# New product orders, held first reads, a third seven-product pair in the output projection, and the residual put into PSUM ahead of the products, in a two-layer decoder kernel

## The chip, the cores and the metric

The kernel runs on one core of a Trainium2 chip. The metric is the device time of one execution in microseconds; lower is better. Five engines are named in the profile: PE (TensorE, the matrix products, with its weight loads as PEld), DVE (VectorE), ACT (ScalarE), POOL (GpSimd) and SP (SyncE, which only issues DMA here). Each engine takes its instructions in order.

## What is computed

Two identical layers act on x, 256 rows (tokens) by 2048 columns, all in float32. Cut to what matters:

```
def hybrid_layer(x, ...):
    h = rms_norm(x, attn_norm)
    proj = h @ w_in                        # 2048 x 6160
    g_q, g_k, g_v, g_gate, g_lr, s_q, s_k, s_v = split(proj)
    o_gla = rms_norm(gla_chunked(g_q, g_k, g_v, gates(g_lr))) * silu(g_gate)
    o_sb  = rms_norm(stick_breaking_attention(rms_norm(s_q), rms_norm(s_k), s_v))
    x = x + concat(o_gla, o_sb) @ w_o      # 2048 x 2048
    hm = rms_norm(x, mlp_norm)
    up = square(relu(hm @ w_up))           # 2048 x 8192
    return x + up @ w_down                 # 8192 x 2048
```

Nearly all arithmetic is in w_in, w_o, w_up and w_down.

## The kernel before

**Three matmuls for one product.** Every float32 operand is split into a high part (rounded to the fp32r format that the matmul takes) and a low part (the value less its high part). A product is high*high + high*low + low*high, so three matmuls of 128x512 columns (lines 1198 to 1200, `product`). For the weights, ACT rounds (line 1066, `whi`) and DVE subtracts (line 1070, `wlo`).

**Units and pairs.** A unit is 1024 output columns (512 for the unit "g"). Its contraction is walked in eight "pairs" of two 128-row blocks. The results of a unit are four 128x512 blocks (two token halves, two column halves), and an ordinary pair takes eight products into PSUM banks 2, 4, 3 and 8. A "fast" pair takes seven, by a Strassen-Winograd scheme into all eight banks (1, 5, 6, 7 as well): it needs sums of weight blocks (DVE, line 858: `ts` and two sums in place in `raw`) and sums of activation blocks (`forms`, lines 454 to 475, tiles `sx`, `sxh`). At the end of a unit its tail folds the banks together: `up_tail` into new tiles, `down_tail` into the residual `xb`.

**The sequence.** Layer 0 begins with a first stretch that is written in the order of program text: x is loaded and turned, and a unit of lines 594 to 615 (`whi`, `wlo`, `acc`) makes the GLA values. Then three units ("iv", "ik", "iq") make projections for layer 0. In each layer follow attention (lines 613 to 1780), then the units g, o 0, o 1, and for q = 0 to 3: up 0, up 1, down 0, down 1. In layer 0 iv, ik and iq of layer 1 come last. All units from iv on are placed by `ordered`.

**How weights come in.** Most pairs come as one 1 MB read that SP issues (line 1002, `raw`, three buffers). The "added" pairs (third entry of an order, two of a unit) come instead in two halves, each read twice by DMAs that POOL issues: line 1033 reads 512 KB into `chi`, rounding on the way (three buffers, `CAST`); ACT writes minus that into `dlo` (line 1037, `negated`, two buffers, `ADDS`); line 1040 reads the same weights again and adds them into `dlo`. So an added half needs no DVE work, one ACT instruction, and two reads. A half is started one half ahead of its use (`AHEAD_BY`).

**What sets the order.** An order is a list of pair numbers, one entry per step (a fast pair has four steps of 2, 2, 2 and 1 products, an ordinary pair two of 4; a half of an added pair is a step of 4), with the fast pairs and the added pairs beside it. PE follows these lists. For the other engines a planner (`Plan`) holds costs and due times: PE pieces are laid end to end, each other piece is due as late as its users allow, and a clock is run in which an engine that is free takes, of the pieces that are ready, the one due first. The order that comes out is the written order of PE, DVE and ACT. The planner's `LAND` is 7.0 for a read and its `ADD` 6.0 for the adding read. The dummy pieces `before` (five PE pieces of twelve matmuls) stand for work ahead of the first unit, and the copies `copy_first` (line 903), which empty the accumulator of the unit before, wait for the fourth of them.

**The lines that the prediction uses.** Line 500 writes the high part of turned x, line 563 is a warming transpose, line 490 turns x, line 334 turns the gains that line 500 scales by, line 1292 applies relu, line 1311 turns the result of an up unit for the down unit.

Of the kernel before, what the change touches and what calls it, by code (L numbers as in the profile page):

```python
# [17 lines left out]
P = 128  # L18
# [1 line left out]
WARM0, WARM1 = 8, 13  # L20
T2 = 5
FAST = (1, 3, 5, 6)
EACH = [0, 0, 1, 1, 1, 1, 2, 3, 3, 3, 3, 2, 5, 5, 5, 5, 4, 6, 6, 6, 6, 4, 7, 7], FAST, (2, 4)
FEWER = [0, 0, 1, 1, 1, 1, 2, 3, 3, 3, 3, 2, 5, 5, 4, 6, 6, 6, 6, 4, 7, 7], (1, 3, 6), (2, 4)
FAST_OF = {"sxh": (0, 1, 3, 5, 6), "sx": FAST}
TWO_WAYS = (("sxh", 0),)
MORE = [0, 0, 0, 0, 2, 1, 1, 1, 1, 2, 3, 3, 3, 3, 4, 5, 5, 5, 5, 4, 6, 6, 6, 6, 7, 7], (0, 1, 3, 5, 6), (2, 4)
# [135 lines left out]
def trunk_kernel(  # L163
# [51 lines left out]
    def act_tile(dt, shape=(P, 4, T)):  # L215
        return apool.tile(list(shape), dt, tag="act", name=nm("act"))
# [29 lines left out]
    def bank(m):  # L246
        return unused.pop(m, None) or new_bank(m)
# [191 lines left out]
    def forms(op, i, t, tag):  # L439

        both = (tag, i) in TWO_WAYS
        keep = tag is None or both

        e = []
        todo = []

        def sums():
            a11, a21, a12, a22 = (t[:, k, r * P : (r + 1) * P] for k in range(2) for r in range(2))  # L450
            n = 4 if keep else 3
            e.append(tmp("t2", [P, 512], bufs=T2)[:, : n * P].rearrange("p (k c) -> p k c", c=P))
# [4 lines left out]
            nc.vector.tensor_tensor(e[0][:, 1, :], a12, e[0][:, 0, :], ALU.subtract)  # L457

        def high():
            if e:  # L460
                if both:
                    op.x[i] = tmp(tag + "k", [P, 4, 2, P], F32R, bufs=1)
                elif keep:
                    op.x[i] = act_tile(F32R, (P, 4, 2, P))
                else:
                    op.x[i] = tmp(tag, [P, 3, 2, P], F32R, bufs=len(FAST))
                todo.append((op.x[i], e[0]))
            if i not in op.t:
                todo.append((op.pair(i), t))
            for d, src in todo:  # L470
                nc.scalar.activation(d[:, :, 0, :], src, AF.Copy)
# [370 lines left out]
    def ordered(l, units, hT, rst, ug, gates_t, mixed=None, ons=None):  # L842
# [22 lines left out]
        def unit_order(u):  # L865

            kind, q, n2 = units[u]
            if kind == "g":
                return [i // 2 for i in range(8)], (), ()
            if kind == "o":  # L870
                pairs = ((4, 5, 6, 7, 0, 1, 2, 3), (4, 5, 6, 0, 7, 1, 2, 3))[n2]
                return [j for j in pairs for _ in range(4 if j < 2 else 2)], (0, 1), ()
            if u and units[u - 1][0] == "down" and kind == "iv":
                return FEWER
            return OWN.get((kind, n2, q), OWN.get((kind, n2), EACH))

        def added(u, j):
# [143 lines left out]
        def rounded(u, j, s):  # L1021

            box = {}
            sl = slice(s * 512, (s + 1) * 512)
            src = weights(u, j)[:, :, sl] if by_columns(u, j) else weights(u, j)[:, s : s + 1, :]

            def flat(key):
                t = box[key].rearrange("p c n -> p (c n)")
                return t.rearrange("p (k n) -> p k n", k=src.shape[1])

            def high():
                box["h"] = tmp("chi", [P, 2, 512], F32R, bufs=CAST)
                nc.gpsimd.dma_start(flat("h"), src)  # L1033

            def negated():
                box["l"] = tmp("dlo", [P, 2, 512], F32R, bufs=ADDS)
                nc.scalar.activation(box["l"], f32(box["h"]), AF.Copy, scale=-1.0)  # L1037
# [46 lines left out]

        last = {}
        sums13 = []
        chi, late, made_halves = [], [], {}
        every = [
            (u, k, j, order[:k].count(j))
            for u in range(len(units))  # L1090
# [15 lines left out]
        def added_steps(u, j):  # L1106

            kind, q, _ = units[u]
            op = {"up": hm, "down": up.get(q)}.get(kind, hT)

            def blk(k, tt):
                sl = slice(tt * P, (tt + 1) * P)
                return lambda: (op.t[j][:, k, 0, sl], op.t[j][:, k, 1, sl])

            for s in range(2):
                if by_columns(u, j):
                    prods = [
                        (m, [(blk(k, tt), k) for k in range(2)])
                        for tt, m in enumerate(((2, 4), (3, 8))[s])
                    ]  # L1120
                else:
                    prods = [
                        (m, [(blk(s, tt), c)])
                        for c, ms in enumerate(((2, 4), (3, 8)))
                        for tt, m in enumerate(ms)
                    ]
                yield prods

        def steps(u, j, is_fast, r, ld, readers):
# [14 lines left out]
                        for tt, m in enumerate((1, 6))]  # L1144
                return

            kept = kind in AHEAD or ({"up": "sxh", "down": "sx"}.get(kind), j) in TWO_WAYS

            def ext(i):
                return lambda: (op.x[j][:, i, 0, :], op.x[j][:, i, 1, :])  # L1150
# [36 lines left out]
                (4, [(blk(1, 1), 0)]),  # L1187
            ]

        def product(m, blocks, box, begin, end):  # L1190

            if begin:
                banks[m] = bank(m)
            for i, (a, c) in enumerate(blocks):
                ah, al = a()
                h, lo = box["h"][:, c], box["l"][:, c]
                o = banks[m]
                nc.tensor.matmul(o, ah, h, start=begin and i == 0, stop=False)
                nc.tensor.matmul(o, ah, lo, start=False, stop=False)  # L1199
                nc.tensor.matmul(o, al, h, start=False, stop=end and i + 1 == len(blocks))  # L1200

        def bk(m):
            return lambda: banks[m]


        def down_tail(u):
# [43 lines left out]
                x_done[2 * n2 + c] = got  # L1250

            return sums, half

        def up_tail(u):
            kind = units[u][0]
# [154 lines left out]
        def turn_gated():  # L1410

            g, cost, turn, a, m, e, high, low, scaled, box = turns.pop(0)
            p = add("PE", cost, turn, a, free[m])
            if e < 2:
                b = add("ACT", A1, scaled, p, take=1)
                free[m] = [b]
                done["o", 0, e] = made(lambda: forms(mixed, e, box[1], "sx"), True, True, b)
            else:
                b = add("ACT", A1, high, p)
                done["o", 0, e] = add("DVE", 0.7, low, b)  # L1420
                free[m] = [b, done["o", 0, e]]
# [30 lines left out]
            gate(0)  # L1452
        for u, (kind, q, n2) in enumerate(units):
            order, quick, by_dma = unit_order(u)
            if kind != "g":
# [9 lines left out]
            for k, j in enumerate(order):  # L1465
# [10 lines left out]
                for m, blocks in prods:  # L1476
                    begin, end = m not in begun, last_use[m] == k
                    begun.add(m)
                    p[m] = add(
                        "PE", 3 * MM * len(blocks),  # L1480
                        lambda a=(m, blocks, box, begin, end): product(*a),
                        h, lo, ready, free[m] if begin else [], opened if u == 0 else [],
                    )
                    for tile_users in users:
                        tile_users.append(p[m])
                if kind == "g" and k == 4 or kind == "o" and n2 == 0 and k == 5:
# [356 lines left out]
```

## Time and profile before

| | |
|---|---|
| time, median of 3 runs | 2147.89 us (2144.24 to 2151.99) |
| the profiled execution's own time | 2145.96 us, span 2144.3 us |
| PE busy | 2124.8 us, 10076 matmuls |
| PEld busy | 1765.1 us |
| DVE busy | 1944.5 us, 2636 instructions |
| ACT busy | 1403.3 us |
| POOL busy | 234.5 us |
| DMA | 488.74 MB, 228 GB/s |
| mean granted TensorE clock | 0.997 |

Busy time is the time in which at least one instruction of the engine was in flight. Matmuls overlap, so a busy PE is not yet a PE that loses nothing: what counts is the distance from one matmul's start to the next. In rows of the timeline the first number is the start in us from the span's start, the second the duration, and the bracket names how long the engine had been idle and what released it. In tables by stretch of time each engine's busy us and count stand under its name, then the granted clock, the share of the DMA engines that was busy, and GB/s.

### The profile page before, as it was taken

To read this page: it belongs to the slowest core of one execution; us is meant where nothing else is said; L and a number is where in the kernel's file an instruction comes from. 1 tells how busy PE (TensorE), PEld (TensorE's weight loads), DVE (VectorE), ACT (ScalarE), POOL (GpSimd) and SP (SyncE) were. 2 spreads that over 40 slices of the span, in tenths; PEclk is the share of its full clock that TensorE was granted. 3 is DMA by queue.
4 is the path that set the end of the run, shared out by engine and by line. 5 is a ranking of instruction groups with operands and counts; after the bars stand their busy time and mean duration, and the time that the engine had idled before them with its cause. 6 is when DMAs were issued, how large, how long until landed. Compare 5 with 4: busy or idle time off the path is not lost.

```text
span 2144.3 us, 28255 instructions
## 1 busy us (share of the span) xinstructions
PE 2124.8 (99%) x10076; PEld 1765.1 (82%) x10076; DVE 1944.5 (91%) x2636; ACT 1403.3 (65%) x1853; POOL 234.5 (11%) x362
## 2 busy tenths in 40 slices
PE   8999999999999999999999999999999999999999
PEld 6788888888888888888888988888888888888887
DVE  5988878999999999999999796699999999999998
ACT  6666666676577566667766575666765765765764
POOL 0110000011111111111111100000111111111110
PEclk9999999999999999999999999999999999999999
DMA  7885365588888988988888644756888888888886
GB/s 247 245 236 179 118 187 196 167 246 252 258 251 246 268 239 253 266 245 238 252 258 251 191 138 137 224 162 204 260 241 258 254 258 247 246 255 256 248 244 196
DMA packets 146992, 488.74 MB, mean 228 GB/s; under 512 B 10298, under 2 KB 19074, under 8 KB 146852
## 3 DMA queue, kind: packets, MB, share of 16 engines
q1 hardware_dynamic: 103076, 327.55, 44.7%
q0 software_dynamic: 43776, 159.40, 31.6%
q8 instruction: 79, 1.29, 0.2%
q14 instruction: 61, 0.50, 0.1%
HBM read 484.81 MB, written 2.10 MB: 227 GB/s over the span
## 4 chain that ended last, share of the span: by engine, by line
PE 55%; issue 36%; POOL 5%; DMA 2%; DVE 1%; ACT 1%; POOLq 0%
POOL dlo L1040 3%; PE acc L613 3%; PE acc L615 2%; PE acc L614 2%; POOL chi L1033 2%; DMA dlo<-in_w_up_dram 1%; DMA dlo<-in_w_in_dram 1%; DMA dlo<-in_w_down_dram 1%; PE ps L1780 0%; DVE wlo L596 0%; DMA chi<-in_w_in_dram 0%; PE ps L724 0%; PE ps L1730 0%; PE ps L1773 0%; PE ps L778 0%
## 5 line engine op out<-in xcount | busy, mean ns | idle before, releaser
L1066 ACT ACTIVATE whi<-raw 128x1024 fp32r<-128x1024 f32 (+1 forms) x701 | 653.2, 955 | 364.6 <-DVE raw L858 209.9
L1070 DVE TENSOR_TENSOR wlo<-raw,whi 128x1024 fp32r<-128x1024 f32 (+1 forms) x701 | 760.9, 1091 | 70.0 <-ACT whi L1066 21.7
L1037 ACT ACTIVATE dlo<-chi 128x1024 fp32r<-128x1024 f32 x152 | 159.9, 1053 | 83.0 <-DMA chi<-in_w_in_dram 13.9
L1066 ACT ACTIVATE whi<-ts 128x1024 fp32r<-128x1024 f32 x165 | 174.4, 1057 | 53.5 <-DVE ts L858 29.2
L858 DVE TENSOR_TENSOR ts<-raw 128x1024 f32<-128x1024 f32 x165 | 200.7, 1216 | 3.9 <-DMA raw<-in_w_down_dram 2.2
L1070 DVE TENSOR_TENSOR wlo<-ts,whi 128x1024 fp32r<-128x1024 f32 x165 | 200.8, 1217 | 0.4 <-PE m__631_2940 L1199 0.2
L613 PE MATMUL acc<-whi,act 128*128 128x512 f32 (+2 forms) x384 | 142.1, 370 | 2.6 <-ACT whi L594 2.6
L615 PE MATMUL acc<-whi,act 128*128 128x512 f32 (+2 forms) x384 | 137.6, 358 | 0.0
L614 PE MATMUL acc<-wlo,act 128*128 128x512 f32 (+2 forms) x384 | 137.4, 358 | 0.0
L594 ACT ACTIVATE whi<-raw 128x1024 fp32r<-128x1024 f32 (+2 forms) x98 | 88.1, 906 | 64.7 <-PE acc L615 64.3
L596 DVE TENSOR_TENSOR wlo<-raw,whi 128x1024 fp32r<-128x1024 f32 (+2 forms) x98 | 100.4, 1030 | 30.4 <-ACT whi L594 29.5
L1033 POOL DMA_DIRECT2D chi<-in_w_up_dram x64 | 35.4, 555 | 759.2 <-PE m__2836_13416 L1200 142.1
L858 DVE TENSOR_TENSOR raw<-raw 128x512 f32<-128x512 f32 x165 | 112.8, 684 | 1.3
L858 DVE TENSOR_TENSOR raw<-ts,raw 128x512 f32<-128x512 f32 x165 | 112.5, 682 | 0.1
L1033 POOL DMA_DIRECT2D chi<-in_w_down_dram x64 | 35.4, 554 | 524.2 <-PE m__3624_17092 L1200 33.1
L1292 ACT ACTIVATE act<-act,st 128x512 f32<-128x512 f32 x88 | 60.5, 715 | 46.5 <-DVE act L858 46.4
L613 PEld LDWEIGHTS acc<-whi,act 128*128 128x128 f32 x384 | 72.9, 190 | 15.3 <-issue 3.4
L615 PEld LDWEIGHTS acc<-whi,act 128*128 128x128 f32 x384 | 72.9, 190 | 10.6
L614 PEld LDWEIGHTS acc<-wlo,act 128*128 128x128 f32 x384 | 73.0, 190 | 9.3 <-DVE wlo L596 0.4
L1040 POOL DMA_DIRECT2D dlo<-in_w_down_dram x64 | 54.7, 854 | 68.4 <-ACT dlo L1037 66.0
L475 DVE TENSOR_TENSOR act<-t,act 128x512 fp32r<-128x512 f32 x90 | 61.1, 682 | 0.0
L1040 POOL DMA_DIRECT2D dlo<-in_w_up_dram x64 | 54.8, 856 | 56.7 <-ACT dlo L1037 55.4
(4156 smaller groups left out, 5738.9 us busy)
## 6 DMA issues: line engine op xcount, KB each, us to landing
raw<-in_w_up_dram SPq DMA_DIRECT2D x96, 1024.0 KB, 7.8
raw<-in_w_down_dram SPq DMA_DIRECT2D x96, 1024.0 KB, 10.0
raw<-in_w_in_dram SPq DMA_DIRECT2D x72, 1024.0 KB, 5.3
chi<-in_w_up_dram POOLq DMA_DIRECT2D x64, 512.0 KB, 5.6
dlo<-in_w_up_dram POOLq DMA_DIRECT2D x64, 512.0 KB, 8.5
raw<-in_w_o_dram SPq DMA_DIRECT2D x32, 1024.0 KB, 5.2
chi<-in_w_down_dram POOLq DMA_DIRECT2D x64, 512.0 KB, 5.9
dlo<-in_w_down_dram POOLq DMA_DIRECT2D x64, 512.0 KB, 10.0
```

Of the source, the lines that this page charges most:

```text
L475: nc.vector.tensor_tensor(d[:, :, 1, :], src, f32(d[:, :, 0, :]), ALU.subtract)
L594: newest["hi"] = nc.scalar.activation(h, r, AF.Copy).ins
L596: newest["lo"] = nc.vector.tensor_tensor(lo[:, q : q + step, :width], r, f32(h), ALU.subtract).ins
L613: nc.tensor.matmul(o, xh[:, sl], whi[:, j, :width], start=first, stop=False)
L614: nc.tensor.matmul(o, xh[:, sl], wlo[:, j, :width], start=False, stop=False)
L615: st["mm"] = nc.tensor.matmul(o, xl[:, sl], whi[:, j, :width], start=False, stop=last).ins
L858: nc.vector.tensor_tensor(dst, a, b, op)
L1033: nc.gpsimd.dma_start(flat("h"), src)
L1037: nc.scalar.activation(box["l"], f32(box["h"]), AF.Copy, scale=-1.0)
L1040: nc.gpsimd.dma_start(flat("l"), src, accum_op=ALU.add)
L1066: nc.scalar.activation(box["h"][:, :n], src(), AF.Copy)
L1070: nc.vector.tensor_tensor(box["l"][:, :n], src(), f32(box["h"][:, :n]), ALU.subtract)
```

## The change

Five things are edited.

- **Orders.** `EACH`, `FEWER` and the lists of up 0, up 1, down 0 and down 1 are written anew, each unit with its own, and `LATER` is new, for ik and iq of layer 1. Fast pairs are interleaved with others, and the added halves are spread differently. The number of fast and of added pairs is as before in all of these units.
- **The output projection.** `O0` and `O1` give the o units three fast pairs (0, 1, 2) in place of two, and two added pairs in place of none.
- **Held first reads.** Ahead of layer 0 the first three `chi` tiles are first touched by ACT (`held_tile`, one column, from `ident`), so their reads wait for that instruction; and in the planner each `chi` read waits for the first product of the unit before its own (`started`). That second edit adds no wait on the chip; it moves the read, and what follows it, in the written order.
- **Seeding.** In down 0, down 1 and o 1 ACT copies the four residual blocks into banks 2, 4, 3 and 8 (`seed`) once the unit before has emptied them; the products are added on top, the first without a start flag. The tail (`seeded_tail`) has eight DVE instructions where `down_tail` had twelve, and five ACT instructions where it had one.
- **Planner costs** are changed by a few per cent.

```diff
-EACH = [0, 0, 1, 1, 1, 1, 2, 3, 3, 3, 3, 2, 5, 5, 5, 5, 4, 6, 6, 6, 6, 4, 7, 7], FAST, (2, 4)
+EACH = [7, 7, 5, 2, 5, 5, 1, 1, 5, 4, 1, 1, 3, 3, 3, 3, 4, 6, 6, 2, 6, 6, 0, 0], FAST, (2, 4)
...
-OWN = {("up", 0): MORE, ("up", 0, 0): EACH}
+O0 = [6, 6, 7, 4, 5, 4, 0, 0, 1, 0, 7, 0, 1, 1, 1, 5, 2, 2, 2, 2, 3, 3], (0, 1, 2), (5, 7)
+O1 = [5, 7, 7, 0, 0, 0, 1, 0, 6, 1, 1, 2, 1, 2, 2, 2, 5, 3, 6, 3, 4, 4], (0, 1, 2), (5, 6)
+SEEDED = (("down", 0), ("down", 1), ("o", 1))
+SPARE = ()
+OWN = {
+    ("up", 0): ([4, 0, 0, 0, 0, 1, 1, 2, 1, 1, 6, 6, 2, 6, 6, 5, 5, 5, 5, 4, 3, 3, 3, 3, 7, 7], (0, 1, 3, 5, 6), (2, 4)),
...
+    ("up", 1): ([0, 0, 3, 3, 3, 3, 2, 1, 1, 1, 2, 1, 5, 5, 5, 4, 6, 5, 6, 6, 6, 7, 4, 7], FAST, (2, 4)),
+    ("down", 0): ([0, 0, 3, 3, 1, 2, 3, 3, 1, 1, 5, 1, 4, 5, 5, 5, 2, 6, 6, 6, 6, 7, 7, 4], FAST, (2, 4)),
+    ("down", 1): ([0, 0, 5, 5, 4, 5, 5, 6, 6, 6, 4, 6, 3, 3, 3, 1, 2, 3, 1, 1, 1, 2, 7, 7], FAST, (2, 4)),
+}
...
-        MM, TR, V2, V1, A2, A1 = 0.227, 0.108, 1.15, 0.61, 1.0, 0.55
+        MM, TR, V2, V1, A2, A1 = 0.2268, 0.109, 1.15, 0.62, 1.06, 0.60
...
             if kind == "o":
-                pairs = ((4, 5, 6, 7, 0, 1, 2, 3), (4, 5, 6, 0, 7, 1, 2, 3))[n2]
-                return [j for j in pairs for _ in range(4 if j < 2 else 2)], (0, 1), ()
+                return (O0, O1)[n2]
...
+            def held_tile():
+                box["h"] = tmp("chi", [P, 2, 512], F32R, bufs=CAST)
+                nc.scalar.activation(box["h"][:, 0, :1], ident[:, :1], AF.Copy)
+
...
-            h = add("POOL", 1.0, high, chi[-CAST] if len(chi) >= CAST else [], lag=LAND)
+            first = None
+            if l < 0 and len(chi) < CAST:
+                first = add("ACT", 0.2, held_tile, before[0])
+            h = add(
+                "POOL", 1.0, high, first, chi[-CAST] if len(chi) >= CAST else [],
+                started[u - 1] if u else [], lag=LAND,
+            )
...
-            if begin:
+            if begin and m not in seeded:
                 banks[m] = bank(m)
...
+                nc.tensor.matmul(
+                    o, ah, h, start=begin and i == 0 and m not in seeded, stop=False, **check
+                )
...
+        def seed(m, x):
+            banks[m] = bank(m)
+            nc.scalar.activation(banks[m], x(), AF.Copy)
+
+        def seeded_tail(u):
...
+            seeds = {
+                m: add("ACT", A1, lambda m=m, x=x: seed(m, x), free[m], gate_done[0, 1], x_done.get(2 * n2 + c))
+                for m, x, c in ((2, x11, 0), (4, x21, 0), (3, x12, 1), (8, x22, 1))
+            }
...
-            if e < 2:
+            if e in O0[1] + O1[1]:
...
                         h, lo, ready, free[m] if begin else [], opened if u == 0 else [],
+                        seeds.get(m) if begin else [],
```

More of the change, by code (lines that the diff above doesn't have):

```diff
@@ L1086, in ordered @@
         sums13 = []
-        chi, late, made_halves = [], [], {}
+        chi, late, made_halves, started = [], [], {}, {}
         every = [
@@ L1108, in added_steps @@
             kind, q, _ = units[u]
-            op = {"up": hm, "down": up.get(q)}.get(kind, hT)
+            op = {"o": mixed, "up": hm, "down": up.get(q)}.get(kind, hT)
             def blk(k, tt):
@@ L1145, in steps @@
                 return
-            kept = kind in AHEAD or ({"up": "sxh", "down": "sx"}.get(kind), j) in TWO_WAYS
+            kept = kind in AHEAD or ({"up": "sxh", "down": "sx", "o": "sx"}.get(kind), j) in TWO_WAYS
             def ext(i):
@@ L1188, in steps, with product @@
             ]
-        def product(m, blocks, box, begin, end):
-            if begin:
+        def product(m, blocks, box, begin, end, seeded):
+            if begin and m not in seeded:
                 banks[m] = bank(m)
@@ L1197, in product @@
                 o = banks[m]
-                nc.tensor.matmul(o, ah, h, start=begin and i == 0, stop=False)
-                nc.tensor.matmul(o, ah, lo, start=False, stop=False)
-                nc.tensor.matmul(o, al, h, start=False, stop=end and i + 1 == len(blocks))
+                check = dict(skip_group_check=True) if m in seeded else {}
+                nc.tensor.matmul(
+                    o, ah, h, start=begin and i == 0 and m not in seeded, stop=False, **check
+                )
+                nc.tensor.matmul(o, ah, lo, start=False, stop=False, **check)
+                nc.tensor.matmul(
+                    o, al, h, start=False, stop=end and i + 1 == len(blocks), **check
+                )
         def bk(m):
@@ L1454, in ordered @@
             order, quick, by_dma = unit_order(u)
-            if kind != "g":
+            seeds = {}
+            if (kind, n2) in SEEDED:
+                seeds, *tails[u] = seeded_tail(u)
+            elif kind != "g":
                 tails[u] = (down_tail if kind in ("o", "down") else up_tail)(u)
@@ L1480, in ordered @@
                         "PE", 3 * MM * len(blocks),
-                        lambda a=(m, blocks, box, begin, end): product(*a),
+                        lambda a=(m, blocks, box, begin, end, seeds): product(*a),
                         h, lo, ready, free[m] if begin else [], opened if u == 0 else [],
+                        seeds.get(m) if begin else [],
                     )
+                    started.setdefault(u, p[m])
                     for tile_users in users:
```

53 lines of the change are left out of this document (49 added, 4 removed).

## The prediction

> **What bounds the kernel now.** I read the page's first part, then busy time by stretches, since shares are means over unlike stages.
>
> ```profile
> PE 2124.8 (99%) x10076; PEld 1765.1 (82%) x10076; DVE 1944.5 (91%) x2636; ACT 1403.3 (65%) x1853; POOL 234.5 (11%) x362
> ...
> 12.00:18.00 6.00, 4.09 (x9) 2.97 (x10) 4.15 (x8) 4.24 (x10) 0.88 (x1) 0.50 1.07 318
> 30.00:50.00 20.00, 20.00 (x93) 16.33 (x92) 14.58 (x20) 14.71 (x30) 0.00 (x0) 1.00 0.58 189
> 400.00:1150.00 750.00, 748.58 (x3387) 620.20 (x3386) 722.18 (x933) 502.15 (x630) 98.53 (x140) 1.00 0.84 248
> 1400.00:2140.00 740.00, 738.52 (x3335) 611.12 (x3332) 706.86 (x905) 481.49 (x594) 86.77 (x123) 1.00 0.81 239
> ```
>
> In the two long stretches PE is idle 1.4 us of 750 and 1.5 of 740, at full clock, with DVE at 96%. Busy PE proves little, so next came the starts of matmuls in the timeline, in the opening and in an undisturbed place:
>
> ```profile
> 15.66 0.63 PE L613 MATMUL acc<-whi,act 128*128 128x512 f32 x1
> 16.09 0.63 PE L614 MATMUL acc<-wlo,act 128*128 128x512 f32 x1
> ...
> 412.45 0.39 PE L1198 MATMUL m__813_3884<-whi,act 128*128 128x512 f32 x1
> 412.68 0.39 PE L1199 MATMUL m__813_3884<-wlo,act 128*128 128x512 f32 x1
> ```
>
> At full clock matmuls start 0.227 us apart (412.45 to 412.68) though each is shown 0.39 long; at the half clock of the opening it is 0.43. The 0.227 is PE's real pace: where it holds, only fewer matmuls make the kernel faster. So I looked for where it doesn't hold, in PE's waits:
>
> ```profile
> PE acc L613 <- ACT whi L594: 2.6, 1, 2.6
> ...
> PE m__3833_18093 L1199 <- DMA dlo<-in_w_up_dram: 1.2, 1, 1.2
> ...
> PE m__156_800 L1199 <- DMA dlo<-in_w_in_dram: 0.9, 1, 0.9
> PE ps L490 <- DMA xb<-in_x_dram: 0.8, 1, 0.8
> PE m__626_2935 L1199 <- DVE wlo L1070: 0.8, 1, 0.8
> PE m__2637_12424 L1199 <- DVE wlo L1070: 0.8, 1, 0.8
> PE m__80_434 L1199 <- DVE wlo L1070: 0.6, 3, 0.2
> PE m__1598_7549 L1199 <- DMA dlo<-in_w_down_dram: 0.4, 1, 0.4
> PE m__893_4268 L1199 <- DMA dlo<-in_w_up_dram: 0.4, 1, 0.4
> PE m__1681_7936 L1199 <- DMA dlo<-in_w_down_dram: 0.4, 1, 0.4
> PE m__3694_17427 L1199 <- DMA dlo<-in_w_down_dram: 0.3, 1, 0.3
> PE m__1063_5046 L1199 <- DMA dlo<-in_w_down_dram: 0.2, 1, 0.2
> ```
>
> That is little: 2.9 us for `dlo` in the MLP units, 0.9 for it ahead of layer 0, 0.8 at the first product of each layer's unit g, some in the opening. DVE at 96% hardly makes PE wait, so taking DVE work away is worth nothing in itself.
>
> **The third fast pair.** Seven products for eight, three matmuls each, in four o units: 4 x 3 x 0.227 = **-2.7 us**. PE is the pace there, so this is kept unless a new wait eats it. What is added (sums of weights on DVE, forms of pair 2, halves of the two added pairs) is off PE.
>
> **First negations of a layer.**
>
> ```profile
> 1356.12 1.99 ACT L1037 ACTIVATE dlo<-chi 128x1024 fp32r<-128x1024 f32 x2
> 1358.02 1.04 ACT L1066 ACTIVATE whi<-raw 128x1024 fp32r<-128x1024 f32 x1
> 1359.09 1.23 DVE L1070 TENSOR_TENSOR wlo<-raw,whi 128x1024 fp32r<-128x1024 f32 x1 [1.56 <-ACT whi L1066]
> 1359.12 0.50 PE L1198 MATMUL m__2637_12424<-whi,act 128*128 128x512 f32 x1
> 1360.38 0.50 PE L1199 MATMUL m__2637_12424<-wlo,act 128*128 128x512 f32 x1 [0.76 <-DVE wlo L1070]
> ```
>
> Two negations, wanted only units later, stand on ACT ahead of g's first rounding; then DVE's low part, then PE. From start to start PE loses 1360.38 - 1359.12 - 0.23 = 1.03 us, and the list of waits has the same 0.8 us of idle PE for layer 0 (bank 626). With `started` the planner may not read those tiles before g's first product, so the negations go behind the rounding. Rounding 1.9 us sooner covers 1.03 whole: 2 x 1.03 = **-2.1 us**. It would be 0 if the `raw` read lands only then; ACT's idle time was not put down to it.
>
> **The opening.**
>
> ```profile
> 1.36 0.69 POOL L1033 DMA_DIRECT2D chi<-in_w_in_dram  x1 [0.33 <-issue]
> 8.75 0.19 DVE L335 COPY gcol_a<-ps 128x32 f32<-128x32 f32 x1 [8.75 <-PE ps L334]
> 10.83 1.06 ACT L1037 ACTIVATE dlo<-chi 128x1024 fp32r<-128x1024 f32 x1 [1.51 <-DMA chi<-in_w_in_dram]
> 11.79 1.55 ACT L500 ACTIVATE act<-ps,gcol_a 128x256 fp32r<-128x256 f32 x4
> 13.22 2.20 ACT L594 ACTIVATE whi<-raw 128x512 fp32r<-128x512 f32 x4
> 13.91 0.79 PE L613 MATMUL acc<-whi,act 128*128 128x512 f32 x1 [2.63 <-ACT whi L594]
> 42.40 0.60 ACT L903 ACTIVATE act<-acc 128x512 f32<-128x512 f32 x1 [3.59 <-PE acc L615]
> 42.89 1.05 ACT L1066 ACTIVATE whi<-raw 128x1024 fp32r<-128x1024 f32 x1
> ```
>
> Line 500 could run once the gains are there (8.75 + 0.19), but ACT stands in a negation that waits for `chi`: 11.79 - 9.0 = 2.8 us. The held write (0.2 on ACT's empty start) matters less for when the read begins, about 1 us, than for order. On the planner's clock the held write can go after one dummy of twelve matmuls (12 x 0.2268 + 0.06 = 2.78), so the read has landed at 2.78 + 0.2 + 0.06 + 1.0 + 7.06 = 11.1; iv's first rounding is ready at 2.9 + 7.06 = 9.96, the first copy of line 903 after four dummies, at 10.95, and due before the second rounding: so the order becomes rounding, copy, negation, copy, next rounding, and the negation moves behind 42.4. That frees the head: -2.6 (the first wait of PE, if `raw` is there), and up to -0.8 for x, because two adding reads and the third `chi` (1.5 MB) leave a stretch with the DMA share above 1: -3.4 at best. What is late next: the negation now stands ahead of iv's second rounding, so that starts 1.5 us after its old place (1.06 of negation, 0.5 of copy): about +1.4. And its adding read is issued at about 44.3 for a half wanted 10 products x 0.68 = 6.8 us after iv begins, 8.2 with that wait; landing took
>
> ```profile
> DMA to landing us min/median/max: 5.4/9.6/12.4
> ```
>
> so, counted from iv's beginning, with 0.5 of copy, 1.06 of negation and 0.3 to hand over it is there at 1.9 + 5.4 = 7.3 at best and 11.5 at the median: +0 to +3.3. The DMA share is 0.58 there, nearer an empty machine, so +1.1. Sum **-0.9** (-3.4 to +1.3).
>
> **Waits for added halves.** An adding read can begin when the half two before it is used up. In the old list of four fast pairs, 18 products lie between (4 fast steps, a half, 4 fast steps), 12.2 us, twice in a unit; in the new lists one such distance a unit is 17 to 19 products (up 1: 17, up 0: 18, down 0 and 1: 19), the others 21 to 40. Negation (1.06) and the median landing (9.6 from the issue) fill 10.7 us of it, and with the longest landing, 12.4, it is 13.5: the old waits are the tail of the landing times, met in two places a unit. Half of these places are left, so half the loss: 2.9 us and 0.2 for each of six restarts (1.03 lost against 0.8 idle, above) are 4.1, half is **-2.0** (0 to -4.1). Ahead of layer 0 the same with 0.9 + 0.6 and four restarts, 2.3: **-1.1** (0 to -2.3).
>
> **Seeding.** Costed at nothing, with the cover named. At the boundary up 1 / down 0:
>
> ```profile
> 495.28 0.69 DVE L858 TENSOR_TENSOR act<-m__896_4280,act 128x512 f32<-128x512 f32 x1
> 496.00 0.73 ACT L1292 ACTIVATE act<-act,st 128x512 f32<-128x512 f32 x1 [0.67 <-DVE act L858]
> 496.63 1.05 ACT L1066 ACTIVATE whi<-raw 128x1024 fp32r<-128x1024 f32 x1
> 497.70 0.39 PE L1198 MATMUL m__983_4672<-whi,act 128*128 128x512 f32 x1
> ...
> L471 ACT ACTIVATE act<-t 128x512 fp32r<-128x512 f32 x90 | 55.9, 625 | 5.2 <-DVE t L457 4.2
> ```
>
> Bank 4 (896) is emptied at 495.97 and wanted by 983 at 497.70: 1.73 us. No ACT instruction of before writes PSUM; the nearest rows are 0.60 (line 903, out of PSUM) and 0.73 (line 1292), so I take 0.63, the 128x512 copy. With one rounding (1.05) in progress ahead of it, 1.68 just fits; that is the hiding place, and the new lists, which end in 7, 4, 7 or 7, 7, 4, leave banks 2 and 4 longer still. 72 seeds of 0.63 are 45 us of an engine that is 65% busy; DVE loses as many of 0.68. If the cover is gone, every further instruction ahead shows on PE in full, and all that stands behind the seed on ACT, roundings first, waits too. For such small misses in 18 seeded and all reordered units: **+0.6** (0 to +18, the upper end below).
>
> **Sum.** -2.7 - 2.1 - 0.9 - 2.0 - 1.1 + 0.6 = -8.2: the profiled execution's own 2145.96 (span 2144.3 and 1.7 around) becomes 2137.8. The median of the three runs, 2147.89, lies 1.9 higher, so **2139.7**.
>
> **Rivals.**
>
> *All waits go.* -2.7 - 2.1 - 3.4 - 4.1 - 2.3 = -14.6: 2133.3. For it: DVE gets room, and each wait has one cause. Against it: the opening's new order of ACT. The opening may give more: the clock is 0.50 from 12 to 18 with matmuls 0.43 apart, and PE was idle in front; were it to come up 5 us sooner, 12 matmuls x 0.2 = 2.4 more, 2130.9. The Trainium skill, "TensorE: Matmul & The Clock Gate", "What's actually happening", says that the gate opens after one busy window of some 3.4 us; by that rule work that follows the warming transposes without a hole would bring it; the trace agrees so far that the slow stretch follows an idle one.
>
> *Only the products.* Waits change places (the read of iv's first half, new lists with a half at step 0 in up 0): -2.7, 2145.2, the same within error. For it: landing times scatter from 5.4 to 12.4, whatever the list.
>
> *The seed decides (slower).* Emptying bank, seed and first product are strictly in a row on one bank. With two roundings ahead of the seed, 2 x 1.05 + 0.63 = 2.73 against 1.73: 1.0 us at each of 18 boundaries, +18, and -8.8 of the rest: +9.2, 2157.1. It decides from 8.8/18 = 0.5 us a boundary. For it: 1.73 has no room. Against: the planner puts what is due first. The Trainium skill, "PSUM — Partial Sum Buffer", "Terms", says that two engines must not touch a bank's quadrant at once, so no step of that row can overlap the next; the trace agrees, it shows DVE begin only after the bank's last product.
>
> **Chances.** The sum 0.50 (own range 2135 to 2145; two thirds of it below the bound), all waits 0.20, only the products or as much given back 0.20, slower by seeds 0.10. What this kernel's measurement can tell is about 0.3%, 6.4 us: faster means below 2141.5, slower above 2154.3. Faster 0.33 + 0.20 = 0.53; slower 0.10; same 0.37. Range 2131 to 2148: all waits with the clock at one end; at the other the unknown costs of opening and halves taken at their worst, the full seeding case left out.
>
> **What would show it.** Right: PE runs 12 matmuls fewer; no L1037 ahead of L500 and first L613 near 11.3; no wait at the first L1199 of g; fewer `dlo` waits. Wrong: PE waits on an ACT write of a bank at starts of down units; a wait of iv's second step or first half above 3 us; ACT idle on DVE in front of seeds.

## The result, and the profile after

The changed kernel takes 2134.01 us (median of four runs, 2132.97 to 2134.52) against 2146.40 of the kernel before on the same chip (2144.24 to 2151.99): a ratio of 0.9935, interval 0.9919 to 0.9952. It is faster by 12.4 us; 8.2 were forecast. The profiled execution's own time went from 2145.96 to 2134.41, by 11.55. Note the spread: 1.6 us for the runs of after, 7.8 for those of before.

Busy time on the page of after, and in the same stretches as before, the last one cut at 2128 (PE, PEld, DVE, ACT, POOL, then granted clock, DMA share, GB/s):

```profile
PE 2120.0 (99%) x10064; PEld 1763.6 (83%) x10064; DVE 1909.1 (90%) x2578; ACT 1452.1 (68%) x1940; POOL 276.4 (13%) x394
```

```profile
12.00:18.00 6.00, 5.32 (x22) 4.03 (x21) 2.08 (x4) 3.24 (x8) 0.00 (x0) 0.74 1.05 397
400.00:1150.00 750.00, 749.57 (x3395) 622.19 (x3395) 701.89 (x893) 521.60 (x662) 108.43 (x143) 1.00 0.86 251
1400.00:2128.00 728.00, 727.98 (x3292) 604.18 (x3291) 683.31 (x864) 501.34 (x627) 103.41 (x135) 1.00 0.85 247
```

PE runs exactly 12 matmuls fewer, as reckoned. In the long stretches its idle time fell from 1.4 and 1.5 us to 0.4 and 0.0. PE's waits on other engines and DMAs in the trace of after:

```profile
PE acc L626 <- ACT whi L607: 1.6, 1, 1.6
...
PE m__229_1148 L1224 <- DVE act L871: 1.1, 1, 1.1
...
PE m__82_434 L1227 <- DVE wlo L1095: 0.8, 1, 0.8
PE m__851_4026 L1224 <- DVE act L519: 0.4, 1, 0.4
PE m__82_434 L1224 <- ACT whi L1091: 0.3, 1, 0.3
```

The rows left out are of the first 30 us (transposes, the first unit) and of attention. No row names `dlo` any more, none names unit g's first product, and none an ACT write of a bank. In their place stand two rows on bank 82 (the second step of iv), one on bank 229 and one on 851 (the start of up 0).

To see where the time came from I compared the start of the same matmul in both traces: the first and last product, and the marks between them that stand for a stage (first product of iv, first of attention, the transposes of line 1311, 1395 in after, with which the first up 1 of a layer begins). Four of these rows, first in before (its first product is at 13.91), then in after:

```profile
42.20 0.39 PE L1198 MATMUL m__82_436<-whi,act 128*128 128x512 f32 x1
...
455.75 0.60 PE L1311 MATMUL m__899_4292<-ident,act 128*128 128x128 f32 x4
...
2139.77 0.39 PE L1200 MATMUL m__4010_18908<-whi,act 128*128 128x512 f32 x1
```

```profile
10.26 0.51 PE L626 MATMUL acc<-whi,act 128*128 128x512 f32 x1 [1.56 <-ACT whi L607]
38.29 0.39 PE L1224 MATMUL m__80_432<-whi,act 128*128 128x512 f32 x1
...
451.31 0.60 PE L1395 MATMUL m__908_4324<-ident,act 128*128 128x128 f32 x4
...
2128.20 0.39 PE L1228 MATMUL m__4024_18956<-whi,act 128*128 128x512 f32 x1
```

| mark | lead of after, us |
|---|---|
| first product (13.91 before) | 3.65 |
| iv begins | 3.91 |
| attention of layer 0 begins | 3.48 |
| first up 1 of layer 0 begins | 4.44 |
| attention of layer 1 begins | 7.06 |
| first up 1 of layer 1 begins | 8.64 |
| last product | 11.57 |

So 3.9 come ahead of iv, -0.4 in iv, ik and iq, 1.0 and 1.6 in g, the o units and the first up 0 of the two layers, and 2.6 + 2.9 = 5.5 in the MLP units (with the next layer's projections).

### The profile page after: what moved, and what is told of

Its sections match the earlier page's. It is cut to its first block, busy times and chain, and to the rows that moved or that the text cites. A ratio compares the mean times of both kernels' runs of the same rounds, so it can differ in the third digit from the quotient of the medians.

```text
span 2132.7 us, 28217 instructions
## 1 busy us (share of the span) xinstructions
PE 2120.0 (99%) x10064; PEld 1763.6 (83%) x10064; DVE 1909.1 (90%) x2578; ACT 1452.1 (68%) x1940; POOL 276.4 (13%) x394
## 4 chain that ended last, share of the span: by engine, by line
PE 94%; DVE 3%; DMA 2%; ACT 1%; issue 1%; SPq 0%; ACTq 0%; DVEq 0%
PE acc L626 3%; PE acc L628 3%; PE acc L627 3%; DVE wlo L1095 1%; DMA xb<-in_x_dram 1%; DMA raw<-in_w_up_dram 1%; DMA raw<-in_w_in_dram 1%; PE ps L1869 0%; PE ps L1862 0%; DVE wlo L609 0%; PE ps L737 0%; PE ps L1819 0%; DVE ts L871 0%; PE ps L791 0%; PE ps L755 0%
## 5 line engine op out<-in xcount | busy, mean ns | idle before, releaser
L1095 DVE TENSOR_TENSOR wlo<-raw,whi 128x1024 fp32r<-128x1024 f32 (+1 forms) x689 | 744.0, 1089 | 86.2 <-ACT whi L1091 39.8
L1091 ACT ACTIVATE whi<-raw 128x1024 fp32r<-128x1024 f32 (+1 forms) x689 | 644.7, 950 | 185.8 <-DVE raw L871 67.6
L1056 ACT ACTIVATE dlo<-chi 128x1024 fp32r<-128x1024 f32 x168 | 177.6, 1057 | 117.7 <-DMA chi<-in_w_o_dram 5.1
L1091 ACT ACTIVATE whi<-ts 128x1024 fp32r<-128x1024 f32 x169 | 179.0, 1059 | 89.9 <-DVE ts L871 42.2
L871 DVE TENSOR_TENSOR ts<-raw 128x1024 f32<-128x1024 f32 x169 | 206.1, 1220 | 6.3 <-DMA raw<-in_w_o_dram 2.4
L1095 DVE TENSOR_TENSOR wlo<-ts,whi 128x1024 fp32r<-128x1024 f32 x169 | 206.1, 1220 | 4.1 <-ACT whi L1091 4.1
L1059 POOL DMA_DIRECT2D dlo<-in_w_down_dram x64 | 60.1, 940 | 51.6 <-ACT dlo L1056 48.1
```

The costliest lines, as they stand in the source:

```text
L871: nc.vector.tensor_tensor(dst, a, b, op)
L1091: nc.scalar.activation(box["h"][:, :n], src(), AF.Copy)
L1095: nc.vector.tensor_tensor(box["l"][:, :n], src(), f32(box["h"][:, :n]), ALU.subtract)
```

## The experiments

Kernel medians are of four runs unless said; each ratio is against the kernel before on the same chip, whose medians were 2147.53, 2145.72 and 2147.63 in the three groups of runs. "Above" and "below after" compare medians of different chips, and the intervals reach some 3.5 us to each side, so differences of 1 to 2 us rest on the traces, not on these times. Numbers of lines are those of the kernel in question.

### What holds the head of the kernel

The first two take the hold apart: without it, and with its place in the planner but not the write on the chip.

```diff
# e1: no hold at all
-            if l < 0 and len(chi) < CAST:
+            if False:
# e2: the planner's piece stays, ACT writes nothing
-                first = add("ACT", 0.2, held_tile, before[0])
+                first = add("ACT", 0.2, None, before[0])
```

> The changed kernel without the held first tiles: the first chi reads go out at once and the two first negations stand on ACT ahead of the first copies of turned x, as before. Theory (the opening's 3.7 us come from the hold: ACT out of a negation and x ahead of the reads): first product back near 13.9, the copy out of the first accumulator near 42.4 instead of 38.5, but iv's second rounding on time, so its wait of 1.5 us is gone: 2134.0 + 3.9 - 1.5 = 2136.4. Rival (the opening gained by the new orders or by chance): first product near 10.3 and 2134.

> The planner still sees the hold, so the negations keep their late place on ACT, but no held write is issued: the first two reads go out at 1.4 and 2.4 us. Tells the two halves of the hold apart. Theory (what counted was ACT's place; the read's start about 1 us): first product near 11.3, first copy near 39.5, 2135.0. Rival (the reads in front of x and the gains are the whole of it): first product near 13.9, 2137.5. Other rival (the reads' start is worth nothing): 10.3 and 2134.0.

Measured: e1 2136.36 (2135.74 to 2136.82), ratio 0.9942 (0.9923 to 0.9962), 2.4 above after. e2 2132.99 (2131.99 to 2133.40), 0.9927 (0.9911 to 0.9943), 1.0 below it. ACT's timeline in e1, after and e2, ahead of the first product:

```profile
7.88 1.06 ACT L1056 ACTIVATE dlo<-chi 128x1024 fp32r<-128x1024 f32 x1 [5.78 <-DMA chi<-in_w_in_dram]
10.62 1.06 ACT L1056 ACTIVATE dlo<-chi 128x1024 fp32r<-128x1024 f32 x1 [1.69 <-DMA chi<-in_w_in_dram]
11.59 1.55 ACT L513 ACTIVATE act<-ps,gcol_a 128x256 fp32r<-128x256 f32 x4
```

```profile
2.11 0.39 ACT L1047 ACTIVATE chi<-ident 128x1 fp32r<-128x1 f32 x3
6.32 1.57 ACT L513 ACTIVATE act<-ps,gcol_a 128x256 fp32r<-128x256 f32 x4 [3.83 <-DVE gcol_a L345]
9.58 0.63 ACT L607 ACTIVATE whi<-raw 128x512 fp32r<-128x512 f32 x1 [1.69 <-DMA raw<-in_w_in_dram]
```

```profile
7.10 1.56 ACT L513 ACTIVATE act<-ps,gcol_a 128x256 fp32r<-128x256 f32 x4 [5.00 <-DVE gcol_a L345]
```

With the negations ahead of L513 (e1), ACT stands 5.8 and 1.7 us for their reads. Without the write but with the order (e2), L513 stands in front all the same. So the gain is that of ACT's order; that the reads begin later is worth nothing at the first product, as the second rival had it. iv begins 1.0 us earlier in e2 than in after, and in the two profiled runs the clock accounts for it: the granted clock is 1.00 through the whole first unit of e2 and 0.50 from 11.65 to 15.07 in after, and by the twelfth matmul e2 is 0.9 ahead. That the held write costs anything is not shown. e1's iv begins 4.0 us later than that of after, its attention only 1.9: with the negations done early, nothing stands in front of iv's second rounding.

Next the hold alone, put into the kernel before:

```diff
+            def held_tile():
+                box["h"] = tmp("chi", [P, 2, 512], F32R, bufs=CAST)
+                nc.scalar.activation(box["h"][:, 0, :1], ident[:, :1], AF.Copy)
...
-            h = add("POOL", 1.0, high, chi[-CAST] if len(chi) >= CAST else [], lag=LAND)
+            if l < 0 and len(chi) < CAST:
+                first = add("ACT", 0.2, held_tile, before[0])
+            h = add("POOL", 1.0, high, first, chi[-CAST] if len(chi) >= CAST else [], lag=LAND)
```

> The kernel before with the held first tiles alone (old orders, no seeds). Theory: first product near 10.3, first copy near 38.5 (-3.9), and the negation again in front of iv's second rounding (+1.5): about -2.4, 2143.5 against a profiled 2145.96. Rival (the hold works only with the new order of iv): no change.

Measured: 2145.16 (ten runs, 2143.84 to 2150.17), ratio 0.9995 (0.9983 to 1.0007). The time alone decides nothing, since the interval holds the forecast (0.9989) as well as no change. The profiled runs tell more: iv begins 3.73 us earlier than in before and attention 2.22 earlier, as the theory had it, so the hold doesn't need the new order of iv. At 620 us the lead was 3.43; by the last product it was 0.0. PE's list of waits shows where it went:

```profile
PE m__3833_18096 L1207 <- DMA dlo<-in_w_up_dram: 1.3, 1, 1.3
PE m__1372_6494 L1207 <- DMA dlo<-in_w_down_dram: 1.3, 1, 1.3
PE m__3076_14540 L1207 <- DMA dlo<-in_w_down_dram: 1.3, 1, 1.3
```

The same code, somewhat earlier, met more late reads than before had: 5.4 us of `dlo` waits in the MLP units against 2.9. A gain of 2 us at the head can't be read off the end while the units behind it lose a few us to reads that land late.

Last, the copies of line 917 go behind the fifth dummy of the planner in place of the fourth, so that the second rounding of iv keeps its place:

```diff
-                "ACT", A1, lambda tt=tt: copy_first(tt), before[-2], gate_done.get((0, 0))
+                "ACT", A1, lambda tt=tt: copy_first(tt), before[-1 if l < 0 else -2], gate_done.get((0, 0))
```

> The changed kernel, with the two copies out of the first accumulator planned after the fifth dummy piece in place of the fourth (ahead of layer 0 alone), so iv's second rounding and the first negation stand on ACT before them, in the 3.6 us in which ACT waits for the accumulator. Theory (iv's wait of 1.5 us is ACT's order and nothing else): both waits at 41.5 and 42.8 go, 2132.5. Rival (DVE is late in iv anyway, so PE waits elsewhere): 2134.0 with the waits moved to later low parts of iv.

Measured: 2130.90 (2130.20 to 2131.24), ratio 0.9917 (0.9901 to 0.9934), 3.1 below after. ACT at the beginning of iv, in after and in e8, and PE in after:

```profile
38.49 0.60 ACT L917 ACTIVATE act<-acc 128x512 f32<-128x512 f32 x1 [3.57 <-PE acc L628]
38.99 1.05 ACT L1056 ACTIVATE dlo<-chi 128x1024 fp32r<-128x1024 f32 x1
39.93 0.59 ACT L917 ACTIVATE act<-acc 128x512 f32<-128x512 f32 x1
40.41 1.06 ACT L1091 ACTIVATE whi<-raw 128x1024 fp32r<-128x1024 f32 x1
```

```profile
35.83 1.10 ACT L1056 ACTIVATE dlo<-chi 128x1024 fp32r<-128x1024 f32 x1
36.78 1.11 ACT L1091 ACTIVATE whi<-raw 128x1024 fp32r<-128x1024 f32 x1
38.66 0.60 ACT L917 ACTIVATE act<-acc 128x512 f32<-128x512 f32 x1 [0.77 <-PE acc L628]
```

```profile
40.79 0.39 PE L1228 MATMUL m__81_433<-whi,act 128*128 128x512 f32 x1
41.52 0.49 PE L1224 MATMUL m__82_434<-whi,act 128*128 128x512 f32 x1 [0.35 <-ACT whi L1091]
42.78 0.50 PE L1227 MATMUL m__82_434<-wlo,act 128*128 128x512 f32 x1 [0.77 <-DVE wlo L1095]
```

In after the negation and the rounding queue behind the copy, which waits 3.57 us for the accumulator. In e8 both are done while that wait lasts. PE lost 0.50 + 1.03 = 1.5 us at that step in after and nothing in e8. The wait at bank 229 also fell, from 1.1 to 0.4:

```profile
PE m__228_1147 L1224 <- DVE act L871: 0.4, 1, 0.4
```

Between the start of iv and attention e8 gained 3.1 on before, where after lost 0.4. That is more than the 1.5 expected: the low parts of iv that come late in after between 45 and 66 us, 1.0 us in sum and each too short for the list, are gone in e8 too.

### The MLP waits: lists, halves and seeds

```diff
# e9: the kernel before with the new EACH, FEWER, LATER, OWN and planner costs;
#     no hold, no started, no seeds, o units as before
-EACH = [0, 0, 1, 1, 1, 1, 2, 3, 3, 3, 3, 2, 5, 5, 5, 5, 4, 6, 6, 6, 6, 4, 7, 7], FAST, (2, 4)
+EACH = [7, 7, 5, 2, 5, 5, 1, 1, 5, 4, 1, 1, 3, 3, 3, 3, 4, 6, 6, 2, 6, 6, 0, 0], FAST, (2, 4)
...
# e4: after, but EACH, FEWER, MORE and OWN as in before
-LATER = [0, 0, 4, 1, 1, 1, 1, 3, 3, 4, 6, 6, 3, 6, 3, 6, 2, 5, 5, 5, 5, 2, 7, 7], FAST, (2, 4)
+LATER = EACH
+OWN = {("up", 0): MORE, ("up", 0, 0): EACH}
...
# e3: after without seeds; e10: this and the edit of e4
-SEEDED = (("down", 0), ("down", 1), ("o", 1))
+SEEDED = ()
```

> The changed kernel with the new lists of iv, ik, iq and the MLP units (and the new planner costs) as the only part kept: no hold, no rule on the unit before, no seeds, the o units as before with two fast pairs and no added ones. Theory (the lists are the largest part: old lists put back took 10.5 us): 2134.0 + 2.4 (hold undone) + 1.7 (rule undone) + 1.5 (third pair undone) = 2139.6. Rival (the lists only work with DVE's relief and the hold): 2143 or above, with waits for dlo.

> The changed kernel without seeding: all down and o units use the old tail (twelve DVE instructions), all else as changed. Theory (taking work from DVE is worth nothing while PE keeps its pace): 2134 to 2135, PE's list of waits with at most 1 us more. Rival (the new orders and the added halves only hold because DVE has room): DVE back near 96% of the long stretches, waits of PE on low parts or on emptied banks at unit ends, 5 us or more, 2139 or above.

> The changed kernel with the old lists for iv, ik, iq and all MLP units; o lists, hold and seeds stay as changed. Theory (the waits for added halves came from the old spacing of the halves): PE's waits for dlo come back, 2 to 4 us in all, 2137. Rival 1 (DVE's relief by the seeds removed them): no dlo waits, 2134. Rival 2 (old lists leave a seed too little room, 1.73 us at bank 4): waits of PE on an ACT write at starts of down units, 0.5 us each or more, 2140 or above.

> The run with the old lists, now without seeds as well: 2144.5 with seeds. There PE waited 5.5 us for banks that DVE empties, which the kernel before never did. Theory A (the seeds' four instructions on ACT at unit ends push ACT and then DVE late under the old lists): these waits go, only dlo waits stay, 2139 to 2140. Theory B (late reads of added halves hold ACT, and through it DVE, whatever the seeds): the waits stay, 2144.

| | lists | seeds | median (lowest to highest) | ratio (interval) |
|---|---|---|---|---|
| after | new | yes | 2134.01 (2132.97 to 2134.52) | 0.9935 (0.9919 to 0.9952) |
| e3 | new | no | 2134.45 (2133.15 to 2134.59) | 0.9943 (0.9926 to 0.9959) |
| e4 | old | yes | 2144.52 (2142.09 to 2147.92), ten runs | 0.9995 (0.9986 to 1.0005) |
| e10 | old | no | 2136.56 (2135.06 to 2140.59) | 0.9954 (0.9939 to 0.9969) |
| e9 | new | no, nor hold nor o | 2138.81 (2138.50 to 2139.43) | 0.9962 (0.9947 to 0.9977) |

e9 and e3 came as expected; of e9's lead of 7.5 us at the last product 5.5 come after the first up 1 of layer 0, with no `dlo` row among PE's waits. e4 lost far more than the theory of the halves allowed, and e10 gave 8 of its 10.5 us back: with the old lists the seeds cost 8 us, with the new ones nothing (0.4 the other way, within the scatter). But the trace does not show the rival as it was worded. PE's waits in e4 beyond those of the opening, the largest:

```profile
PE m__3855_18166 L1219 <- DVE act L866: 1.8, 1, 1.8
PE m__1521_7189 L1222 <- DMA dlo<-in_w_up_dram: 1.8, 1, 1.8
```

No row of the list names an ACT seed. The waits are on banks that DVE empties late at the start of up 1 (unseeded), and on `dlo`. What ACT's negations stood waiting for between 400 and 1150 us, in e4's list of ACT's waits:

```profile
ACT dlo L1051 <- DMA chi<-in_w_up_dram: 15.1, 7, 3.4
...
ACT dlo L1051 <- DMA chi<-in_w_down_dram: 5.2, 2, 3.3
```

ACT stands 20 us in negations whose `chi` read has not landed, in front of all it has yet to do. In the same stretch it is 5.1 us in e10 and 5.8 in before.

So the question became whether the distance of the halves, not the interleaving, is what the lists bring. e12 is e4 with only the added halves moved in the old lists, until 25 to 27 products lie between a half and the one two before it:

```diff
-EACH = [0, 0, 1, 1, 1, 1, 2, 3, 3, 3, 3, 2, 5, 5, 5, 5, 4, 6, 6, 6, 6, 4, 7, 7], FAST, (2, 4)
+EACH = [0, 2, 0, 1, 1, 1, 1, 2, 3, 3, 3, 3, 5, 5, 4, 5, 5, 6, 6, 6, 6, 4, 7, 7], FAST, (2, 4)
# FEWER and MORE alike
```

> The run with the old lists, with only the added halves moved: the sequence of the other pairs is the old one, and the four halves of a unit stand evenly, so that from the end of a half to the half two later lie 25 to 27 products everywhere (old: 18 at half of the places; changed kernel: 16 to 19 at a quarter). Theory (the distance of the halves is what makes PE wait for dlo, and late halves drag ACT and the banks): no dlo wait, 2134 to 2136. Rival (the interleaving of the fast pairs is what counts, through DVE and the raw buffers): 2143 to 2145.

Measured: 2137.03 (2136.34 to 2137.28), ratio 0.9952 (0.9936 to 0.9969): 7.5 below e4 with every seed in place, and 1 us above the range of the theory. PE's whole list:

```profile
PE m__80_432 L1222 <- DMA dlo<-in_w_in_dram: 5.0, 1, 5.0
PE ps L498 <- DMA xb<-in_x_dram: 1.9, 3, 1.3
PE ps L571 <- POOL ident masks.py:199: 1.4, 1, 1.4
PE acc L621 <- ACT whi L602: 1.4, 1, 1.4
PE ps L732 <- DVE act L695: 1.1, 2, 0.5
```

Every wait of the MLP is gone, the bank waits of e4 among them; the 5.0 us are new and my own making, a half at step 1 of the first unit, before its read can be there. They cost more than they last: 2.6 us into the wait the granted clock falls to 0.50, from 44.37 to 51.20, so that matmuls still start 0.43 apart for 4 us after it, and iv takes 7.3 us more than its matmuls at 0.227:

```profile
47.73 0.63 PE L1219 MATMUL m__81_433<-chi,act 128*128 128x512 f32 x1
48.16 0.63 PE L1222 MATMUL m__81_433<-dlo,act 128*128 128x512 f32 x1
```

From the first up 1 of layer 0 to the last product e12 gains 8.85 - 1.71 = 7.1 us on before, and after 11.57 - 4.44 = 7.1 (both with layer 1's g and o units, some 1.6, in it). So, with seeds, the distance of the halves is the cause of the MLP gain, and the interleaving of fast pairs isn't needed for it. Without seeds the old distances cost little in this kernel: in the profiled run of e10 the MLP units gain 4.9 us on before, with the old lists, where those of after gain 5.5.

### Single parts

```diff
# e5: O0 and O1 with two fast pairs, pair 2 ordinary
-O0 = [6, 6, 7, 4, 5, 4, 0, 0, 1, 0, 7, 0, 1, 1, 1, 5, 2, 2, 2, 2, 3, 3], (0, 1, 2), (5, 7)
+O0 = [6, 6, 7, 4, 5, 4, 0, 0, 1, 0, 7, 0, 1, 1, 1, 5, 2, 2, 3, 3], (0, 1), (5, 7)
...
# e6: reads do not wait for the unit before
-                started[u - 1] if u else [], lag=LAND,
+                lag=LAND,
```

> The changed kernel with pair 2 of the o units taken as an ordinary pair again (two fast pairs, same added pairs): 12 matmuls more. Theory (third pair worth 2.7 us, of which some 1.3 went into small waits of its own): +1.5 to +2.7, 2136. Rival (the o units gained by their new order, not by the product): +0.3 or less.

> The changed kernel without the planner's rule that a chi read waits for the first product of the unit before. Theory (this rule alone put the layer's first negations behind g's first rounding): the wait of 0.8 at g's first low part comes back in both layers, 2 x 0.8 lost: 2135.7. Rival (the o units' early need of halves, not the rule, moved them): no such wait, 2134.

Measured: e5 2135.51 (2134.46 to 2136.31), ratio 0.9949 (0.9934 to 0.9964), 1.5 above after. e6 2135.74 (2135.23 to 2136.45), 0.9951 (0.9936 to 0.9966), 1.7 above it, and g's waits are back in its list as they stood in before:

```profile
PE m__626_2938 L1227 <- DVE wlo L1095: 0.8, 1, 0.8
PE m__2646_12455 L1227 <- DVE wlo L1095: 0.8, 1, 0.8
```

### A better version

e2 and e8 together: the planner's hold without the write, and the later copies.

> Both gains of the first four runs together: the hold seen by the planner alone (no held write) and the two copies planned after the fifth dummy. Theory (they act at different places, -1.0 before iv and -3.1 in iv): 2129.9. Rival (both take the same time out of the opening): 2130.9 or above.

Measured: 2129.47 (2128.79 to 2130.86), ratio 0.9919 (0.9904 to 0.9934), 4.5 us below after and 0.4 below the theory's sum. Of PE's waits in the units and MLP only one is left:

```profile
PE m__228_1144 L1224 <- DVE act L871: 0.4, 1, 0.4
```

## Why the prediction was right, step by step

The direction, the 12 matmuls and the time within the range came out right; 2134.0 lies 5.7 below the forecast and 0.7 above the rival "all waits go". Against that rival the MLP gave more (5.5 for 4.1), and the opening with iv and the o units gave less. So the time fell into the range although the sum was a third too small, and the rival, given 0.20, lies nearer than the sum, given 0.50.

- **Third fast pair: -2.7 forecast, -1.5 measured.** The 12 matmuls went, but the four o units give 0.43, 0.30, 0.44 and 0.28 by the starts of what follows them, where 0.68 each was reckoned, and e5 puts the price of undoing it at 1.5. The step that failed is "kept unless a new wait eats it": no wait is long enough to be listed there, but the starts show the loss, at one place of each unit: in o 0 two matmuls on bank 691 (337.68 in layer 0) start 0.13 and 0.11 late, in o 1 two on bank 732 (388.33) 0.20 and 0.11, the first of them 0.05 after DVE has ended its `wlo`. Without seeds (e3, e10) o 1 gives the whole 0.68 in both layers, but up 0 behind it then loses 0.6 to 0.8. Besides, a new wait stands in up 0 of layer 0 (bank 851 on DVE line 519, 0.4 idle), and 0.7 us of the lead go there.
- **First negations of a layer: -2.1 forecast, 0.88 + 0.81 = -1.7 measured**, -1.7 by e6. Right by cause and nearly by size.
- **The opening: -0.9 forecast for head, rounding and half together; measured -3.9 and +1.5, so -2.4.** The order of ACT came out as reckoned, instruction by instruction, both in front (no negation ahead of line 513) and at iv (rounding, copy, negation, copy, rounding), and its price of +1.4 measured 1.5. Two terms were mis-sized: the head by 0.5 (-3.4 was "at best"), and the landing of iv's first half (+1.1), which cost nothing: no row names it in after. (The lower end of its range, -3.4, had also left out the price of 1.4.) What I read as two effects, order and a later read, is one: e2 shows that the hold's write isn't needed.
- **Ahead of layer 0: -1.1 forecast.** From iv to attention the lead falls by 0.4; with the rounding's 1.5 set apart that is -1.1. It is right by luck, though. By the starts of the matmuls the waits of before cost 3.5 there, not 2.3; the `dlo` wait (1.2) went whole, of the 2.3 of late low parts 1.0 is left, and the new wait at bank 229 (1.3 with its restart) was not foreseen. e8 has -3.1 there.
- **Waits for added halves in the MLP: -2.0 forecast, -5.5 measured.** This is the term that made the difference of the whole. "Half of these places are left, so half the loss" is the step that failed. All the `dlo` rows went; by the starts of the matmuls they had cost 4.5 in before with their restarts (4.1 was reckoned), and some 1.0 of small restarts went with them. That the distance of the halves decides is right with the seeds in place, as e12 shows, but a loss from the tail of landing times doesn't go by the number of places: the new lists keep one distance of 17 to 19 products a unit, as short as the old 18, and no wait stands there. The loss falls also because the reads themselves land sooner. The adding reads between 400 and 1150 us, in before and then in after:

```profile
DMA to landing us min/median/max: 6.5/9.6/11.6
```

```profile
DMA to landing us min/median/max: 5.4/8.5/11.3
```

  The share of the DMA engines rose meanwhile from 0.84 to 0.86, so it isn't less traffic. That it is traffic spread more evenly is only argued.
- **Seeding: +0.6 forecast, 0 measured under the new lists (e3).** The copy takes 0.57 to 0.60, where 0.63 was taken; one in the table of a line's instructions (ns, shortest, median, longest):

```profile
L1286 ACT ACTIVATE m__984_4664<-xb x1: 582/582/582, 488.0 to 488.0; 128x512 f32<-128x512 f32 x1
```

  From the end of a seed to the first product on its bank 0.34 us are left at least and 2.54 in the median of 72, so the cover named holds. The rival "the seed decides" has the wrong place but a true core: under the old lists seeds cost 8 us, and the trace shows them not between seed and first product, but in banks that DVE empties late and in ACT standing for `chi`; how the seeds lead there is only argued. Had the lists not come with it, the kernel would be no faster than before (e4).
- **The clock.** In the stretch from 12 to 18 it rose from 0.50 to 0.74. In the trace of before it is 0.50 from 9.11 to 19.35, 5.4 us of that behind the first product; in after it is 1.00 at the first product and 0.50 only from 11.65 to 15.07. The last matmul that is followed at half pace (0.42 us later) starts at 18.65 in before and at 14.47 in after; before, then after:

```profile
18.65 0.63 PE L614 MATMUL acc<-wlo,act 128*128 128x512 f32 x1
19.07 0.53 PE L615 MATMUL acc<-whi,act 128*128 128x512 f32 x1
```

```profile
14.47 0.63 PE L627 MATMUL acc<-wlo,act 128*128 128x512 f32 x1
14.89 0.48 PE L628 MATMUL acc<-whi,act 128*128 128x512 f32 x1
```

  So the slow stretch came earlier and was a third as long, but little was gained by it: the lead grows from 3.65 at the first product to 4.18 at the twelfth, and a wait for x takes 0.86 back. That is 0.5 us, not the 2.4 of the rival. The Trainium skill, "TensorE: Matmul & The Clock Gate", "What's actually happening", has the gate open after one busy window of some 3.4 us; the trace agrees: the clock is at half for 3.41 us in after and for 10.24, three times as long, in before.

**What stays open.** With the old lists and no seeds, before and e7 have `dlo` waits and the list of the profiled run of e10 has none (one of its four runs took 2140.59, 3.4 us longer than the next); e10 also has `started`, the new costs and the new o lists, and which of these relieves it was not told apart. So without seeds it isn't shown how much of e9's gain is the lists' and how much that of the planner's costs beside them. What makes the matmuls of o 0 late, and how the seeds lead to late banks under the old lists, was not settled either.

## What to carry to other kernels

A read that is late only now and then costs time at the places in the order that leave it no slack: find the shortest distance between the freeing of a buffer and the use of its next content, in products, and lengthen that one first; in the MLP, with the seeds in place, moving the halves alone was worth as much as all the new lists. On an engine that takes its work in order, an instruction that waits for a transfer costs what stands behind it, so look at what is written ahead of the first work on the critical path, and move that rather than the transfer. An addition that is free in a well-spaced order can cost 8 us in a tight one, so test parts both alone and together.

## What had not been expected of the hardware

- The time that a read takes depends on the order that issues it, with the same reads and bytes. Landings of the adding reads of e4 and then of e12 between 400 and 1150 us:

```profile
DMA to landing us min/median/max: 6.8/9.4/12.7
```

```profile
DMA to landing us min/median/max: 5.8/8.2/11.0
```

  The same split runs through all fourteen kernels: medians of 9.4 to 9.6 us with the old lists (before, e4, e7, e10), 8.2 to 8.7 with the new ones or with the halves spread (e12); for the 1 MB reads into `raw` 8.9 to 9.8 against 7.1 to 7.9. The shortest distance between halves went from 18 products (12.2 us at 0.68 each) to 25 (17.0) from e4 to e12, while the longest landing fell from above that shortest distance to below it.
- Runs of the kernels with the old lists scatter far more: before by 9.9 us in thirteen runs, e7 by 6.3 and e4 by 5.8 in ten, e10 by 5.5 in four, against 0.9 to 2.1 in four runs of each of the ten others.
- During a wait of PE of 5.0 us (e12) the granted clock fell to 0.50, for 6.8 us in all, and the wait cost 7.3 us with that; after waits of up to 1.8 us (e4) it stayed at 1.00.
